# One group of six tiles instead of two in the seven-product form of a feed-forward layer's second product

## The chip, the cores and the metric

The kernel runs on one core of a Trainium2 chip. Each core has a matrix engine (TensorE, PE in the profile; its weight loads are shown apart as PEld), a vector engine (VectorE, DVE), a scalar engine (ScalarE, ACT), GpSimd (POOL) and SyncE (SP). The last two mostly issue DMA transfers here. All engines run their own queue of instructions in order and wait for each other through semaphores. The metric is the device time of one execution in microseconds. In three runs of the kernel before it was 897.86 (median), 897.61 and 958.67.

## What is computed

One layer of a diffusion backbone over 512 latent tokens with 1024 channels and a context of 256 tokens: a normalised and modulated input, a combined projection, a pooling mixer and a two-way chunked recurrent mixer, a gated sum, an output projection, a residual, and then the feed-forward part, in which everything of this case happens:

```python
def _swiglu(h, w_in, w_out):
    g, u = jnp.split(h @ w_in, 2, axis=-1)
    return (jax.nn.silu(g) * u) @ w_out
...
x = x + g1 * mix_lat
x = x + g2 * _swiglu(_modulate(x, norm_ffn[l], sh2, sc2), w_ffn_in[l], w_ffn_out[l])
...
return _rmsnorm(x, norm_final)
```

`h` is 512 x 1024, `w_in` is 1024 x 5632 (gate and up halves of 2816 columns each), `w_out` is 2816 x 1024. The hidden width 2816 makes 22 tiles of 128.

## The kernel before

**Three matmuls for one.** Data are float32. Each operand is split into a rounded high part (a cast on ACT) and the rest (a subtraction on DVE), and a product is made of three matmuls: high by high, high by low, low by high (`mm3`, lines 188 to 190). A token tile is 512 wide; a matmul has 512 or 256 columns.

**Two products.** The first product makes, for a hidden tile j, gate and up values of 128 channels for 512 tokens. The second takes hidden tiles as its contraction and adds `g2` times the sum to the residual `x1` (8 rows of tiles, 128 x 512 each).

**The seven-product form.** `Pair` (line 1066) makes one hidden tile's gate and up values for both token halves as a 2 x 2 block product with seven block multiplications instead of eight. Its weights are loaded as two tiles, `a` (in a buffer `wr`, three of them) and `b` (in a buffer `ur`, two of them), at lines 1018 and 1019; `prepare` makes the split weights of seven block operands: `A11`, `A12`, `A22` (directly, buffers `oh` and `ol`), and the sums `S1`, `S2`, `S3`, `S4` (lines 1049 to 1057, then casts and subtractions into `gh`/`gl` and `wh`/`wl`). For `A12` and `A22`, and for some odd tiles `A11`, the low part is made by a DMA from POOL that adds the weight from DRAM onto the negated high part (line 1036); the last one of a pair is kept as `p["added"]`. Four products are in `front` (A11, S1, S2, A12) and three in `back` (S3, S4, A22). `run` (line 1246) goes through a list of items: the front of an item is interleaved with the back of the one before it, and the next item is prepared meanwhile. One such turn of a `Pair` has seven products of 12 matmuls with 256 columns.

**The seven-product form of the second product.** `Even` and `Odd` (lines 1154 and 1173) are pairs whose results don't become plain hidden tiles: they are combined (`Fed`, buffers `bo`, `nf`, `ev`) into the seven operands that the second product needs. After six such tiles four `Out` items (line 1202) do the second product for two rows each and store the rows, scaled by `g2`, in a DRAM tensor `od` (lines 1236 and 1240).

**The order of the stages in the feed-forward part.** Tiles 0 to 2 are done plainly (class `Half`) in an order written out by hand for TensorE, ACT and DVE (from line 1332). Tile 3 is a `Pair`. Then the plain second product over tiles 0 to 3 (lines 1427 to 1446), whose first three rows are begun while tile 3 is finished; each finished row of `x1` is stored in DRAM (`x1d`) from POOL, since its place in SBUF is used for `Fed`. Then two groups, tiles 4 to 9 and tiles 10 to 15, each three `Even`, three `Odd` and four `Out`. Then six `Pair` items, tiles 16 to 21; during these `x1` comes back from `x1d` on SP's queue (line 1472), and POOL's queue adds the 16 stored rows of both groups to it (line 1477). At last the plain second product over tiles 16 to 21, in token halves, the norm and the output (from line 1508).

**Who sets the order.** Behind the hand-ordered part the order of each engine's queue is made by the compiler's planner from the order in the program, the dependences and its own estimates of durations. `tc.issue_after(ins)` puts the instructions of its block behind `ins` in the queue of their own engine. A planned order isn't changed at run time: an instruction at the head of a queue that waits holds all behind it.

Of the kernel before, what the change touches and what calls it, by code (L numbers as in the profile page):

```python
# [50 lines left out]
def layer_kernel(ctx: ExitStack, tc, xT, cT, w0, w1, wv0, wv, wada_a, wada_b, par, crow, bg, wpool,  # L51
# [4 lines left out]
    pools, homes, stacks = {}, {}, {}  # L56

    shifted = {"ac"}

    def open_pool(name, tags, side="left"):  # L60
        st = ExitStack()
        p = st.enter_context(tc.tile_pool(name=name, bufs=1, side=side, reuse_waits="tile"))
        pools[name] = p
        for t in tags:
            homes[t] = p
        stacks[name] = st

    def close_pool(name):
        stacks.pop(name).close()

    def tl(tag, shape, dtype=F32, bufs=1, align=None):
        cnt[0] += 1
        return homes[tag].tile(shape, dtype, name=f"{tag}_{cnt[0]}", tag=tag, bufs=bufs, align_bytes=align)

    def S(tag, dtype=F32):
        return tl(tag, [P, T], dtype, BUFS[tag], HALFLINE if tag in shifted else LINE)

    ps = ctx.enter_context(tc.tile_pool(name="ps", bufs=4, space=PSUM))
    dram = ctx.enter_context(tc.tile_pool(name="dram", bufs=1, space=DRAM))
# [96 lines left out]
    def split(src, h, l):  # L176
        nc.scalar.copy(h, src)  # L177
        V.tensor_sub(l, src, h.bitcast(F32))  # L178
        return h, l
# [4 lines left out]
    def mm3(dst, wparts, aparts, first=True, last=True, on=False):  # L184

        n = len(wparts)
        for i, ((wh, wl), (ah, al)) in enumerate(zip(wparts, aparts)):
            nc.tensor.matmul(dst, wh, ah, start=first and i == 0, stop=False, skip_group_check=on)  # L188
            nc.tensor.matmul(dst, wh, al, start=False, stop=False, skip_group_check=on)  # L189
            nc.tensor.matmul(dst, wl, ah, start=False, stop=last and i == n - 1, skip_group_check=on)  # L190

    def mm3_low_last(dst, wparts, aparts, first=True, last=True):

        for i, ((wh, _), (ah, al)) in enumerate(zip(wparts, aparts)):
            nc.tensor.matmul(dst, wh, ah, start=first and i == 0, stop=False)  # L195
            nc.tensor.matmul(dst, wh, al, start=False, stop=False)  # L196
        for i, ((_, wl), (ah, _)) in enumerate(zip(wparts, aparts)):
            nc.tensor.matmul(dst, wl, ah, start=False, stop=last and i == len(wparts) - 1)  # L198
# [231 lines left out]

    def queries(h):
        return [conv_part(lat_tile(Q0 + 2 * h + dk), T, 2 * h + dk,
                          [tl("q", [P, T + NEXT], F32R, BUFS["q"], LINE)[:, NEXT:] for _ in range(2)]) for dk in range(2)]

    def keys(h):

# [577 lines left out]
    def prepare(p, wa, wb, n, turns, sent):  # L1014

        a = tl("wr", [P, WMAX], F32, 3)[:, :2 * n]
        b = tl("ur", [P, D], F32, 2)[:, :2 * n]
        nc.sync.dma_start(b, wb)
        p["loaded"] = nc.sync.dma_start(a, wa)

        def tiled(t):
            return t.rearrange("p (k c) -> p k c", c=P) if turns else t

        def parted(t):
            return [tiled(t)[:, e::2] for e in range(2)] if turns else [tiled(t[:, :n]), tiled(t[:, n:])]

        (a11, a12), (a21, a22) = parted(a), parted(b)

        def direct(nm, w, dram):
            h, l = S("oh", F32R)[:, :n], S("ol", F32R)[:, :n]  # L1030
            nc.scalar.copy(tiled(h), w)
            if nm not in sent:
                V.tensor_sub(tiled(l), w, tiled(h).bitcast(F32))
            else:
                nc.scalar.activation(tiled(l), w, AF.Copy, scale=-1.0)  # L1035
                p["added"] = nc.gpsimd.dma_start(tiled(l), dram, accum_op=ALU.add)  # L1036
            p[nm] = ptiles(h, l, 0, n)

        def summed(names, sg, h, l):
            h, l = h[:, :2 * n], l[:, :2 * n]  # L1040
            split(sg, h, l)
            for e, nm in enumerate(names):
                p[nm] = ptiles(h, l, e * n, n)

        yield
        s12 = tl("sg", [P, D], F32, 2, LINE)[:, :2 * n]
        s1, s2 = tiled(s12[:, :n]), tiled(s12[:, n:])
        direct("A11", a11, parted(wa)[0])
        V.tensor_add(s1, a22, a21)
        V.tensor_add(s2, s1, a11)  # L1050
        summed(("S1", "S2"), s12, wide("gh"), wide("gl"))
        yield
        direct("A12", a12, parted(wa)[1])
        yield
        s34 = tl("sg", [P, D], F32, 2, LINE)[:, :2 * n]
        V.tensor_add(tiled(s34[:, :n]), a11, a21)
        V.tensor_add(tiled(s34[:, n:]), s2, a12)
        yield
        summed(("S3", "S4"), s34, *(tl(t, [P, WMAX], F32R, 2, LINE) for t in ("wh", "wl")))
        yield  # L1060
        direct("A22", a22, parted(wb)[1])
        yield
# [3 lines left out]
    class Pair:  # L1066
# [67 lines left out]
            self.done()  # L1134

        def done(self):
            split(self.s, *self.dst)

    class Fed:

# [105 lines left out]
    def run(items, also=lambda it: None):  # L1246

        prev = None
        for it, after in zip(items, items[1:] + [None]):
            f = it.f = it.f or it.front()  # L1250
            if after:
                made(after)
            b = prev.back() if prev else iter(())
            joint = isinstance(it, Out) and not isinstance(prev, Out)
            if not it.begun:
                next(f)
                next(f)
            if joint:
                for _ in b:
                    pass  # L1260
                after.f = after.front()
                next(after.f)
                next(after.f)
                after.begun = True
            next(b, None)
            next(f)
            next(b, None)
            next(f)
            next(b, None)
            also(it)  # L1270
            prev = it
        return prev
# [1 line left out]
    ng2 = small([P, KT], "ng2")  # L1274
    V.tensor_scalar(ng2, g2, -1.0, None, ALU.mult)
    x1d = dram.tile([KT, P, T], F32, name="x1d")
    od = {c0: dram.tile([KT, P, T], F32, name=f"od{c0}") for c0 in (4, 10)}

    for j in range(NW, KT):
        proj_out(j, wo[j], HALF[0])  # L1280
# [120 lines left out]
    def ffn_bank():  # L1401
        turn_[0] += 1
        return banks[turn_[0] % 3]
# [17 lines left out]
    def wchunk(j, c0, c1, dst=None, skip=0, raw=None):  # L1421
        return wload(wffo[j][:, c0 * P:c1 * P], (c1 - c0) * P, dst, skip, raw)[0]
# [1 line left out]

    c1 = NP + 1
    turn_[0] = NP % 3
    for _ in third.f:
        pass  # L1430
    b = third.back()
    next(b)
    next(b)
    wf, af = [], [ffn_bank(), ffn_bank(), banks[3]]
    for j, acc in enumerate(af):
        if j == 2:
            next(b)
        wf.append(wchunk(j, 0, c1, raw=None if j else tl("ur", [P, D], F32, 2)))
        mm3_low_last(acc, wf[j][:NP], act[:NP], last=False)
    for j, acc in enumerate(af):  # L1440
        mm3(acc, wf[j][NP:], act[NP:c1], first=False)
        ffn_out(j, ALL, None, 0, c1, acc)
        nc.gpsimd.dma_start(x1d[j], x1[j])
    for j in range(3, KT):
        ffn_out(j, ALL, wchunk(j, 0, c1), 0, c1)
        nc.gpsimd.dma_start(x1d[j], x1[j])
    close_pool("late4")
    close_pool("late0")
    open_pool("late0", ("bo", "nf", "ev"))
    items, turn = [], itertools.count(NP + 1)  # L1450
    for c0 in (4, 10):
        evens = []
        for j in range(c0, c0 + 6, 2):
            t = next(turn)
            evens.append(Even(j, t, j == c0 + 4, evens[0].turn if evens else t))
            items += [evens[-1], Odd(j + 1, next(turn), evens[-1])]
        items += [Out(j, next(turn), evens, c0, c0 + 6) for j in range(KT // 2)]
    c0, c1 = 16, FT
    plain = [Pair(j, next(turn)) for j in range(c0, c1)]
    back_ = iter(range(KT))  # L1460

    def also(it):
        if it is plain[0]:
            close_pool("late0")
            open_pool("late0", ("act", "before_act", "x1"))
            tl("before_act", [P, NEXT], F32, 1, LINE)
            shifted.add("act")
            x1[:] = [S("x1") for _ in range(KT)]
        elif it in plain:
            with tc.issue_after(plain[min(plain.index(it) + 1, len(plain) - 1)].p["loaded"].ins):  # L1470
                for j in itertools.islice(back_, 2):
                    nc.sync.dma_start(x1[j], x1d[j])
        if it is plain[-2]:
            with tc.issue_after(plain[-1].p["added"].ins):
                for j in range(KT):
                    for c in (4, 10):
                        nc.gpsimd.dma_start(x1[j], od[c][j], accum_op=ALU.add)

    made(items[0])
    for _ in run(items + plain, also=also).back():  # L1480
        pass
    SumSq.banks = banks[4:]

# [136 lines left out]
```

## Time and profile before

The profiled execution took 899.67 us, of which 897.9 lie between its first and its last instruction. Its mean granted TensorE clock is 0.993. Parts of the page and of the views that are used, beside the lines that the prediction shows:

| what | value |
|---|---|
| the three runs, us | 897.61, 897.86, 958.67 |
| the profiled execution, us | 899.67 |
| its span, us | 897.9 |
| matmuls | 6112 |
| DMA over the span | 134.59 MB, mean 150 GB/s |
| DMA share of the 16 engines by SP's queue | 39.0% |
| line 1036 (add of low weights from POOL) | 42 times, 256 KB each |
| line 1477 (add of a stored row to `x1` from POOL) | 16 times, 256 KB each |
| line 1472 (reload of a row of `x1` from SP) | 8 times, 256 KB each, median 8.8 us to landing |

How to read it: lines of the timeline have start, duration, engine, source line, operation, output and inputs, and in brackets the idle time of the engine before it and what ended that time. A line of the waits has the waiting instruction, the one that it waited for, the total in us, how often, and the longest. A line of the windows has, for a stretch, its length, busy time and number of instructions of PE, PEld, DVE, ACT and POOL, the granted clock, the busy share of the DMA engines and GB/s. Matmuls overlap, so their price is the distance from one start to the next, not their duration.

### The profile page before, as it was taken

How to read it: one execution, taken by the hardware profiler on the slowest of the kernel's cores; microseconds unless marked ns; L12 is line 12 of the kernel's file. 1: busy time of each engine (PE TensorE's matmuls, PEld its weight loads, DVE VectorE, ACT ScalarE, POOL GpSimd, SP SyncE). 2: the span in 40 equal slices, each digit the busy share in tenths (PEclk: the TensorE clock that was granted, in tenths of full speed). 3: DMA queues.
4: the chain of work that ended last, by engine and by line, in shares of the span. 5: the costliest groups of instructions: out<-in, count | busy, mean ns of one | idle time of the engine just before them, and what ended most of it. 6: DMA issues, size and time to landing. Idle time of an engine off the chain costs nothing.

```text
span 897.9 us, 15849 instructions
## 1 busy us (share of the span) xinstructions
PE 874.6 (97%) x6112; PEld 805.4 (90%) x6112; DVE 652.8 (73%) x1292; ACT 470.7 (52%) x919; POOL 98.1 (11%) x137
## 2 busy tenths in 40 slices
PE   9999999999999999999999999999999999998896
PEld 8689798899889998889988899879999999998896
DVE  4678677768876788667886659578888788856544
ACT  4454453545445453354545456446757775755442
POOL 0000000110000100001000000031202220221510
PEclk9999999999999999999999999999999999998999
DMA  9863021445352642526354710379637863794862
GB/s 350 317 201 99 25 71 60 164 129 153 106 177 66 194 112 76 191 69 199 98 153 154 276 48 25 94 211 239 142 103 218 218 147 99 223 283 103 181 127 95
DMA packets 48557, 134.59 MB, mean 150 GB/s; under 512 B 5440, under 2 KB 9824, under 8 KB 47456
## 3 DMA queue, kind: packets, MB, share of 16 engines
q1 hardware_dynamic: 38208, 112.06, 39.0%
q0 software_dynamic: 10272, 21.50, 11.7%
q8 instruction: 48, 0.79, 0.3%
q14 instruction: 29, 0.24, 0.1%
HBM read 123.56 MB, written 9.98 MB: 149 GB/s over the span
## 4 chain that ended last, share of the span: by engine, by line
PE 85%; DVE 6%; DMA 3%; ACT 3%; issue 2%; DVEq 0%; SPq 0%; ACTq 0%
PE ps L188 10%; PE ps L189 10%; PE ps L190 10%; PE ps L198 8%; PE ps L195 8%; PE ps L196 8%; PE pat L348 3%; PE ps L579 3%; PE ps L580 3%; PE ps L581 3%; PE pat L189 2%; PE pat L188 2%; PE pat L190 2%; PE pat L793 2%; PE pat L795 2%
## 5 line engine op out<-in xcount | busy, mean ns | idle before, releaser
L195 PE MATMUL ps<-a,wh 128*128 128x512 f32 x272 | 106.5, 392 | 0.0
L196 PE MATMUL ps<-a,wh 128*128 128x512 f32 x272 | 106.3, 391 | 0.0
L158 ACT CAST wh<-wr 128x1024 fp32r<-128x1024 f32 (+3 forms) x69 | 66.7, 969 | 63.4 <-PE ps L196 34.8
L159 DVE TENSOR_TENSOR wl<-wr,wh 128x1024 fp32r<-128x1024 f32 (+3 forms) x69 | 78.2, 1133 | 28.7 <-ACT wh L158 17.5
L198 PE MATMUL ps<-a,wl 128*128 128x512 f32 x272 | 68.0, 391 | 0.0
L196 PEld LDWEIGHTS ps<-a,wh 128*128 128x128 f32 x272 | 51.1, 188 | 10.2
L198 PEld LDWEIGHTS ps<-a,wl 128*128 128x128 f32 x272 | 50.9, 188 | 10.4
L195 PEld LDWEIGHTS ps<-a,wh 128*128 128x128 f32 x272 | 51.1, 188 | 10.1
L188 PE MATMUL ps<-hp,oh 128*128 128x256 f32 x176 | 50.8, 289 | 8.7 <-DVE tmp L1124 8.1
L1036 POOL DMA_DIRECT2D ol<-in_wffi x42 | 37.1, 882 | 146.6 <-ACT ol L1035 61.5
L188 PE MATMUL ps<-hp,gh 128*128 128x256 f32 x176 | 49.8, 283 | 2.9 <-ACT pat L1086 2.9
L190 PE MATMUL ps<-hp,ol 128*128 128x256 f32 x176 | 50.3, 286 | 0.0
L189 PE MATMUL ps<-hp,oh 128*128 128x256 f32 x176 | 50.2, 285 | 0.0
L189 PE MATMUL ps<-hp,gh 128*128 128x256 f32 x176 | 49.0, 278 | 0.0
L190 PE MATMUL ps<-hp,gl 128*128 128x256 f32 x176 | 48.9, 278 | 0.0
L177 ACT CAST gh<-sg 128x1024 fp32r<-128x1024 f32 (+1 forms) x27 | 26.7, 989 | 41.5 <-DVE sg L1050 26.5
L538 DVE SCALAR_TENSOR_TENSOR pb<-pb,crow_s 128x1024 f32<-128x1024 f32 x32 | 39.1, 1239 | 11.9 <-DMA pb<-in_wada_b 11.8
L188 PEld LDWEIGHTS ps<-hp,oh 128*128 128x128 f32 x176 | 34.6, 197 | 9.4 <-DVE tmp L1124 8.5
L793 PE MATMUL pat<-vh,Sp 128*128 128x258 f32 x144 | 41.1, 285 | 0.0
L794 PE MATMUL pat<-vl,Sp 128*128 128x258 f32 x144 | 40.7, 283 | 0.0
L795 PE MATMUL pat<-vh,Sp 128*128 128x258 f32 x144 | 40.7, 282 | 0.0
L178 DVE TENSOR_TENSOR gl<-sg,gh 128x1024 fp32r<-128x1024 f32 (+1 forms) x27 | 30.9, 1145 | 11.6 <-ACT gh L177 11.6
(422 smaller groups left out, 3031.2 us busy)
## 6 DMA issues: line engine op xcount, KB each, us to landing
wr<-in_w SPq DMA_DIRECT2D x42, 512.0 KB, 3.6
pb<-in_wada_b SPq DMA_DIRECT2D x32, 512.0 KB, 4.3
wr<-in_wffi SPq DMA_DIRECT2D x25, 512.0 KB, 4.8
ol<-in_wffi POOLq DMA_DIRECT2D x42, 256.0 KB, 5.8
ur<-in_wffi SPq DMA_DIRECT2D x19, 512.0 KB, 4.2
ada<-in_wada_a SPq DMA_DIRECT2D x8, 1024.0 KB, 9.9
wr<-in_wffo SPq DMA_DIRECT2D x16, 384.0 KB, 5.2
wr<-in_wout SPq DMA_DIRECT2D x8, 512.0 KB, 3.7
```

Of the source, the lines that this page charges most:

```text
L158: nc.scalar.copy(wh, raw[:, :n])
L159: V.tensor_sub(wl, raw[:, :n], wh.bitcast(F32))
L188: nc.tensor.matmul(dst, wh, ah, start=first and i == 0, stop=False, skip_group_check=on)
L189: nc.tensor.matmul(dst, wh, al, start=False, stop=False, skip_group_check=on)
L190: nc.tensor.matmul(dst, wl, ah, start=False, stop=last and i == n - 1, skip_group_check=on)
L195: nc.tensor.matmul(dst, wh, ah, start=first and i == 0, stop=False)
L196: nc.tensor.matmul(dst, wh, al, start=False, stop=False)
L198: nc.tensor.matmul(dst, wl, ah, start=False, stop=last and i == len(wparts) - 1)
L538: V.scalar_tensor_tensor(wa[:, :D], wa[:, :D], 0.5, crow_s, ALU.mult, ALU.mult, accum_out=mods[:, i:i + 1])
L793: nc.tensor.matmul(o, sh_, vh[:, s, :], start=n == 0, stop=False)
L794: nc.tensor.matmul(o, sh_, vl[:, s, :], start=False, stop=False)
L795: nc.tensor.matmul(o, sl_, vh[:, s, :], start=False, stop=n == len(srcs) - 1)
```

## The change

Only tiles 8 to 13 stay in the seven-product form of the second product. The list of first tiles `starts` has one entry, 8, where `(4, 10)` stood. Tiles 3 to 7 are plain `Pair` items, run through `run` like the later ones, and the first plain block of the second product takes the eight tiles 0 to 7, row after row; rows 0 to 5 of `x1` are stored from POOL as before, rows 6 and 7 from SP, behind the preparation of the first even tile. Tiles 14 to 21 are eight `Pair` items (six before), and the last plain block takes these eight tiles, so that a chunk of weights there is 512 KB (384 before).

The stored rows of the one group are no longer added to `x1` in SBUF after it was loaded. They are added in DRAM, `x1d[j] += od[j]`, by POOL's queue during the later plain pairs: in the turns of the second to the seventh of the eight pairs 1, 2, 2, 1, 1 and 1 rows, each behind the last add of low weights (`added`) of the next pair. The eight loads of `x1` are all put into the turn of the last pair but one, behind that `b` load on SP which belongs to the last pair: `loaded` is now the load of `b`, not of `a`.

In `run`, where the first `Out` follows the last `Odd`, the three back products of the odd tile were done together after the first two products of this `Out`; now they alternate: S3, A11 of `Out`, S4, S1 of `Out`, A22. `done` of a pair writes the cast and the subtraction out, with no other operation.

```diff
-        nc.sync.dma_start(b, wb)
-        p["loaded"] = nc.sync.dma_start(a, wa)
+        p["loaded"] = nc.sync.dma_start(b, wb)
+        nc.sync.dma_start(a, wa)
...
         def done(self):
-            split(self.s, *self.dst)
+            nc.scalar.copy(self.dst[0], self.s)
+            self.over = V.tensor_sub(self.dst[1], self.s, self.dst[0].bitcast(F32))
...
             joint = isinstance(it, Out) and not isinstance(prev, Out)
+            if joint:
+                next(b)
             if not it.begun:
                 next(f)
+                if joint:
+                    next(b)
                 next(f)
             if joint:
-                for _ in b:
-                    pass
+                next(b)
                 after.f = after.front()
...
-    for _ in third.f:
+    starts = (8,)
+    turn = itertools.count(NP + 1)
+    plain = [third] + [Pair(j, next(turn)) for j in range(NP + 1, starts[0])]
+    for _ in run(plain).back():
         pass
-    b = third.back()
-    next(b)
-    next(b)
-    wf, af = [], [ffn_bank(), ffn_bank(), banks[3]]
-    for j, acc in enumerate(af):
-        if j == 2:
-            next(b)
-        wf.append(wchunk(j, 0, c1, raw=None if j else tl("ur", [P, D], F32, 2)))
-        mm3_low_last(acc, wf[j][:NP], act[:NP], last=False)
-    for j, acc in enumerate(af):
-        mm3(acc, wf[j][NP:], act[NP:c1], first=False)
-        ffn_out(j, ALL, None, 0, c1, acc)
-        nc.gpsimd.dma_start(x1d[j], x1[j])
-    for j in range(3, KT):
+    turn_[0] = plain[-1].turn % 3
+    c1 = starts[0]
+    for j in range(KT):
         ffn_out(j, ALL, wchunk(j, 0, c1), 0, c1)
-        nc.gpsimd.dma_start(x1d[j], x1[j])
...
+        if j < KT - 2:
+            nc.gpsimd.dma_start(x1d[j], x1[j])
...
+    c0, c1 = starts[-1] + 6, FT
     plain = [Pair(j, next(turn)) for j in range(c0, c1)]
-    back_ = iter(range(KT))
+    items += plain
+    made(items[0])
+    for j in (KT - 2, KT - 1):
+        nc.sync.dma_start(x1d[j], x1[j])
...
-        elif it in plain:
-            with tc.issue_after(plain[min(plain.index(it) + 1, len(plain) - 1)].p["loaded"].ins):
-                for j in itertools.islice(back_, 2):
+        if it in ins[6:] + plain[1:-1]:
+            after = items[items.index(it) + 1].p.get("added")
+            with tc.issue_after(after.ins) if after else ExitStack():
+                for c, j in itertools.islice(rows, 1 + (it in plain[2:4])):
+                    nc.gpsimd.dma_start(x1d[j], od[c][j], accum_op=ALU.add, max_dma_last_dim=2048)
+        if it is plain[-2]:
+            with tc.issue_after(plain[-1].p["loaded"].ins):
+                for j in range(KT):
                     nc.sync.dma_start(x1[j], x1d[j])
-        if it is plain[-2]:
-            with tc.issue_after(plain[-1].p["added"].ins):
-                for j in range(KT):
-                    for c in (4, 10):
-                        nc.gpsimd.dma_start(x1[j], od[c][j], accum_op=ALU.add)
```

More of the change, by code (lines that the diff above doesn't have):

```diff
@@ L58, in layer_kernel @@
     shifted = {"ac"}
+    bufs = dict(BUFS)
     def open_pool(name, tags, side="left"):
@@ L75, in S @@
     def S(tag, dtype=F32):
-        return tl(tag, [P, T], dtype, BUFS[tag], HALFLINE if tag in shifted else LINE)
+        return tl(tag, [P, T], dtype, bufs[tag], HALFLINE if tag in shifted else LINE)
     ps = ctx.enter_context(tc.tile_pool(name="ps", bufs=4, space=PSUM))
@@ L432, in queries @@
         return [conv_part(lat_tile(Q0 + 2 * h + dk), T, 2 * h + dk,
-                          [tl("q", [P, T + NEXT], F32R, BUFS["q"], LINE)[:, NEXT:] for _ in range(2)]) for dk in range(2)]
+                          [tl("q", [P, T + NEXT], F32R, bufs["q"], LINE)[:, NEXT:] for _ in range(2)]) for dk in range(2)]
     def keys(h):
@@ L1276, in layer_kernel @@
     x1d = dram.tile([KT, P, T], F32, name="x1d")
-    od = {c0: dram.tile([KT, P, T], F32, name=f"od{c0}") for c0 in (4, 10)}
+    od = {c0: dram.tile([KT, P, T], F32, name=f"od{c0}") for c0 in (8,)}
     for j in range(NW, KT):
@@ L1422, in wchunk @@
         return wload(wffo[j][:, c0 * P:c1 * P], (c1 - c0) * P, dst, skip, raw)[0]
-    c1 = NP + 1
-    turn_[0] = NP % 3
-    for _ in third.f:
-        pass
-    b = third.back()
-    next(b)
-    next(b)
-    wf, af = [], [ffn_bank(), ffn_bank(), banks[3]]
-    for j, acc in enumerate(af):
-        if j == 2:
-            next(b)
-        wf.append(wchunk(j, 0, c1, raw=None if j else tl("ur", [P, D], F32, 2)))
-        mm3_low_last(acc, wf[j][:NP], act[:NP], last=False)
-    for j, acc in enumerate(af):
-        mm3(acc, wf[j][NP:], act[NP:c1], first=False)
-        ffn_out(j, ALL, None, 0, c1, acc)
-        nc.gpsimd.dma_start(x1d[j], x1[j])
-    for j in range(3, KT):
-        ffn_out(j, ALL, wchunk(j, 0, c1), 0, c1)
-        nc.gpsimd.dma_start(x1d[j], x1[j])
[L1447 to L1451, printed above, removed]
+    starts = (8,)
+    turn = itertools.count(NP + 1)
+    plain = [third] + [Pair(j, next(turn)) for j in range(NP + 1, starts[0])]
+    for _ in run(plain).back():
+        pass
+    turn_[0] = plain[-1].turn % 3
+    c1 = starts[0]
+    for j in range(KT):
+        ffn_out(j, ALL, wchunk(j, 0, c1), 0, c1)
+        if j < KT - 2:
+            nc.gpsimd.dma_start(x1d[j], x1[j])
+    items, ins = [], []
+    for c0 in starts:
         evens = []
@@ L1455, in layer_kernel @@
             evens.append(Even(j, t, j == c0 + 4, evens[0].turn if evens else t))
-            items += [evens[-1], Odd(j + 1, next(turn), evens[-1])]
+            ins += [evens[-1], Odd(j + 1, next(turn), evens[-1])]
+            items += ins[-2:]
         items += [Out(j, next(turn), evens, c0, c0 + 6) for j in range(KT // 2)]
-    c0, c1 = 16, FT
+    c0, c1 = starts[-1] + 6, FT
     plain = [Pair(j, next(turn)) for j in range(c0, c1)]
-    back_ = iter(range(KT))
+    items += plain
+    made(items[0])
+    for j in (KT - 2, KT - 1):
+        nc.sync.dma_start(x1d[j], x1[j])
+    close_pool("late4")
+    close_pool("late0")
+    open_pool("late0", ("bo", "nf", "ev"))
+    rows = iter([(c, j) for c in starts for j in range(KT)])
     def also(it):
@@ L1467, in also @@
             shifted.add("act")
+            bufs["act"] = 2 * (c1 - c0)
             x1[:] = [S("x1") for _ in range(KT)]
-        elif it in plain:
-            with tc.issue_after(plain[min(plain.index(it) + 1, len(plain) - 1)].p["loaded"].ins):
-                for j in itertools.islice(back_, 2):
-                    nc.sync.dma_start(x1[j], x1d[j])
-        if it is plain[-2]:
-            with tc.issue_after(plain[-1].p["added"].ins):
-                for j in range(KT):
-                    for c in (4, 10):
-                        nc.gpsimd.dma_start(x1[j], od[c][j], accum_op=ALU.add)
-    made(items[0])
-    for _ in run(items + plain, also=also).back():
+        if it in ins[6:] + plain[1:-1]:
[6 more added lines that the diff above has]
+                for j in range(KT):
+                    nc.sync.dma_start(x1[j], x1d[j])
+    for _ in run(items, also=also).back():
         pass
```

## The prediction

> **What bounds the kernel now.** I read the page first (engines, then the chain that ended last), then the list of waits of TensorE in the stretch that the change touches (560 to 856 us: the second half of the feed-forward part), then the timelines around the longest of them.
>
> ```profile
> PE 874.6 (97%) x6112; PEld 805.4 (90%) x6112; DVE 652.8 (73%) x1292; ACT 470.7 (52%) x919; POOL 98.1 (11%) x137
> ...
> PE 85%; DVE 6%; DMA 3%; ACT 3%; issue 2%; DVEq 0%; SPq 0%; ACTq 0%
> ```
>
> TensorE is busy for 97% of the span and holds 85% of the chain. Time is therefore made of two things: how many matmul columns are issued, and the few places where PE stands still. The places, in one view (total us, times, longest):
>
> ```profile
> PE ps L188 <- DVE tmp L1124: 8.1, 2, 4.8
> PE ps L188 <- ACT pat L1086: 2.9, 4, 1.6
> PE ps L188 <- ACT bo L177: 1.2, 2, 0.6
> PE ps L188 <- ACT act L177: 1.2, 1, 1.2
> PE ps L188 <- DVE x L1415: 0.6, 1, 0.6
> ```
>
> That is 14.0 us in 296. Two waits make 8.1 of it, and both are followed by a slow stretch of the TensorE clock:
>
> ```profile
> 812.10:816.10 4.00, 4.00 (x19) 4.00 (x20) 3.51 (x6) 3.77 (x7) 0.72 (x1) 0.50 0.05 3
> 850.60:854.00 3.40, 3.40 (x16) 3.40 (x17) 2.86 (x6) 1.39 (x4) 0.95 (x2) 0.52 1.13 203
> ```
>
> The granted clock (third number from the end) is 0.50 and 0.52 there. Now where those two come from. First wait (SyncE's issues, the chain's DMA piece, VectorE, TensorE):
>
> ```profile
> 790.42 0.33 SPq L1018 DMA_DIRECT2D ur<-in_wffi  x1
> 790.84 3.84 SPq L1472 DMA_DIRECT2D x<-x1d  x6
> ...
> 795.58 0.92 SPq L1472 DMA_DIRECT2D x<-x1d  x2
> 799.35 0.33 SPq L1018 DMA_DIRECT2D ur<-in_wffi  x1
> ...
> 815.11 0.33 SPq L1018 DMA_DIRECT2D ur<-in_wffi  x1
> ```
> ```profile
> 799.35 10.83 DMA ur<-in_wffi
> ...
> 842.21 6.03 DMA wr<-in_wffo
> ```
> ```profile
> 794.47 0.69 DVE L1049 TENSOR_TENSOR sg<-ur 128x512 f32<-128x512 f32 x1 [2.11 <-DMA ur<-in_wffi]
> ...
> 795.81 0.42 DVE L1124 TENSOR_TENSOR tmp<-ps,tmp 128x256 f32<-128x256 f32 x1
> ...
> 810.27 0.69 DVE L1049 TENSOR_TENSOR sg<-ur 128x512 f32<-128x512 f32 x1 [7.75 <-DMA ur<-in_wffi]
> ...
> 811.61 0.42 DVE L1124 TENSOR_TENSOR tmp<-ps,tmp 128x256 f32<-128x256 f32 x1
> ...
> 819.21 0.69 DVE L1049 TENSOR_TENSOR sg<-ur 128x512 f32<-128x512 f32 x1 [0.92 <-DMA ur<-in_wffi]
> ...
> 848.91 0.69 DVE L172 TENSOR_TENSOR ol<-wr,oh 128x512 fp32r<-128x512 f32 x1 [3.93 <-ACT oh L171]
> ...
> 850.12 0.42 DVE L1124 TENSOR_TENSOR tmp<-ps,tmp 128x256 f32<-128x256 f32 x1
> ```
> ```profile
> 797.12 0.28 PE L188 MATMUL ps<-hp,oh 128*128 128x256 f32 x1
> ...
> 806.98 0.28 PE L190 MATMUL pat<-hp,ol 128*128 128x256 f32 x1
> 812.08 0.58 PE L188 MATMUL ps<-hp,oh 128*128 128x256 f32 x1 [4.82 <-DVE tmp L1124]
> ...
> 847.04 0.28 PE L190 MATMUL pat<-hp,wl 128*128 128x256 f32 x1
> 850.59 0.58 PE L188 MATMUL ps<-hp,oh 128*128 128x256 f32 x1 [3.27 <-DVE tmp L1124]
> ```
>
> The eight loads of `x1` go out together; the weight load `ur` behind them (799.35) needs 10.83 us, where one on a calm queue (issued 815.11, used 819.21) needs 4.1. VectorE's queue has L1049, which wants that load for a pair two turns on, ahead of L1124, which the present pair wants before its last product. So a late load of a later pair stops PE. The second wait has the same form: the fifth chunk of the closing weights (842.21) needs 6.03 us while POOL adds the stored rows to `x1`; L172 waits for it, and L1124 behind it.
>
> **The change part by part.** Spacing of matmuls, first and last row of two even stretches:
>
> ```profile
> 590.21 0.39 PE L188 MATMUL ps<-act,wh 128*128 128x512 f32 x1
> ...
> 598.60 0.39 PE L189 MATMUL ps<-act,wh 128*128 128x512 f32 x1
> ...
> 613.95 0.28 PE L188 MATMUL ps<-hp,gh 128*128 128x256 f32 x1
> ...
> 620.77 0.28 PE L188 MATMUL ps<-hp,gh 128*128 128x256 f32 x1
> ```
>
> 37 steps in 8.39 us: 0.227 us for 512 columns. 60 steps in 6.82 us: 0.1137 us for 256.
>
> 1. *Columns.* The first product doesn't change: three plain tiles and 19 in seven-product form both times. The second product of a six-tile group in plain form is 8x6x3 = 144 matmuls of 512 columns, 32.7 us; in seven-product form 4x7x3x3 = 252 of 256, 28.7 us. One group fewer in that form: **+4.0 us**, all on PE, nothing hides it. The first plain block grows from 4 tiles to 8 and the last from 6 to 8, as whole matmuls at the same price per column.
> 2. *First wait.* The reload of `x1` is moved behind the last pair's `b` load, so no pair's load stands behind it. 4.82 us of wait go, and the slow clock after it: 4.00 us for 19 matmuls that take 2.16 at 0.1137, so 1.84. **-6.6 us.** What is late next: a calm load leaves L1124 a margin (done 796.23 against the matmul at 797.12: 0.9 us, the smallest of the plain turns), so this wait goes to nothing.
> 3. *Second wait.* It is 3.27 + (3.40 - 16x0.1137 = 1.58) = 4.9 us. The 16 adds at that place go; in their stretch come eight plain reloads (half the transfers) and chunks of 512 KB instead of 384. A 512 KB load on the calm queue took 4.1 us, under the adds a 384 KB load 6.03: the chunk lands 1.9 us earlier at best. I take a wait of 2.0 that stays (3.27 - 1.9 = 1.4 from this, 0.6 for the reloads still in the queue), and no slow clock, since the 1.6 us wait of the list above is followed by none. **-2.9 us**, between -4.9 (gone) and 0 (as late as now).
> 4. *Entry to the even and odd tiles.* 1.6 (L1086) and 0.6 (L1415) belong to it:
>
> ```profile
> 591.79 7.59 SPq L1019 DMA_DIRECT2D wr<-in_wffi  x3
> ```
>
> The raw buffers of the short 4-tile chunks come free late, so the `a` loads of the first even and odd tile go out only at 591.79, 10 us before they are used. With 8 tiles each chunk has 24x0.227 = 5.4 us of PE time and three raw buffers, so those loads go some 16 us ahead. I take 1.8 of the 2.2 off: **-1.8 us**, between -2.2 and 0. The last two rows of `x1` are stored from SP instead of POOL: each waits for its L1415, and SP's next weight loads queue behind it; if they do so in the wrong order, one load is 4 us late and the gain is lost, hence the 0.
> 5. *Second group's own waits* (one 0.6 at L177, one 0.5 at L1086): **-1.1 us**, between -1.1 and 0.
> 6. *Joint order.* The last odd tile's back products are put between the first ones of `Out`. S3 (12 matmuls, 1.4 us) now stands where PE waits 0.6 for the cast of the last even tile: **-0.6 us**, between -0.6 and +0.6 (S3 is asked for 2 us earlier).
> 7. *Handover to tiles 4 to 7.* The 1.2 us wait (act L177) before the first block goes, since seven tiles (21x0.227 = 4.8 us) cover the last cast. In its place the hand-ordered part ends with a pair whose successor's splits are not done: S1 and S2 need two sums, a cast and a subtraction, some 3.5 us, with two products (2.8 us) before them. **0 us**, between -1.2 and +1.2.
> 8. *Rows added in DRAM.* Nothing like it is in the trace; the nearest is an add into SBUF:
>
> ```profile
> q0 software_dynamic: 10272, 21.50, 11.7%
> ...
> DMA to landing us min/median/max: 4.7/6.8/11.7
> ...
> 825.10:834.70 9.60, 9.60 (x86) 9.60 (x85) 5.13 (x10) 5.40 (x11) 1.75 (x2) 1.00 0.50 96
> ```
>
> By the first row 256 KB of POOL's queue holds the 16 DMA engines for 0.117x897.9/82 = 1.3 us. A turn of a plain pair is 9.6 us with the DMA half idle (0.50), so one row or two (2.6 us) fit. Each is issued behind the pair's own add, and both after that turn's `ur` load. **0 us**, between 0 and +9.8 (third rival).
> 9. *x1[7] on SP.* Its load waits for the last row, issued at the start of the last turn and landed 4.7 to 11.7 us later; the closing chunks queue behind it on SP. Now the fifth chunk goes out at 842.21, some 8 us after the turn starts, because its buffer isn't free earlier; this hides it. Without that cover: the excess of 11.7 over 8, 3.7 us. **0 us.** The longer splits (1.05 and 1.23 us instead of 0.84 and 0.96) lie under 5.4 us of PE per chunk. `done` is the same two instructions written out: 0.
>
> Sum: +4.0 - 6.6 - 2.9 - 1.8 - 1.1 - 0.6 = **-9.0 us**. The profiled execution took 899.67 us (span 897.9), 1.8 above the median of the runs; 890.7 against it is **888.9** against the median 897.86.
>
> **The rivals.** *Both long waits go.* The compiler's planner writes the order outside the hand-ordered part; if L1124 comes ahead of L172, step 3 gives 4.9 and the time is 886.9. For it: the longer chunk arrives later in any plan, so the planner has less reason to put L172 first. Against: it did so before.
>
> *The reload moves the stall.* The change doesn't do what it says: the eight loads of `x1`, 2 MB at once, stand before a closing chunk instead of a pair's load. If that chunk takes the 10.83 us of the load now behind them instead of 6.03, the second wait grows by 4.8 and step 3 gives nothing: 888.9 + 2.9 + 4.8 = 896.6. For it: the same burst did this at 799. Against: most rows are ready early, and the loads can be spread over three turns.
>
> *The rows make each turn's load late.* If the whole engine time of an add falls on the next `ur` load, at 1.9 us each (16 adds in the 30 us that they take now), a turn with one row has L1124 1.9 - 0.9 = 1.0 us late, a turn with two 2.9: 4x1.0 + 2x2.9 = 9.8 us, 898.7 in all, just slower than before. It decides from 1.9 us an add on. Against it: the load at 790.42, with `x1` loads issued 0.4 us behind it, was used at 794.47, as quickly as the calm one. The Trainium skill, "DMA: Bandwidth & Descriptors", section "Queues, rings and completion order", says that each DMA engine goes round the queues that have work, a packet at a time; by that rule POOL's rows would share with SP's load however late they are issued, which is this rival in its mild form. The trace agrees with it only where the queues were full (10.83 us), not at 790.42.
>
> **How the numbers follow.** Forecast 0.5 (888.9), both waits gone 0.2 (886.9), reload moves the stall 0.2 (896.6), rows make loads late 0.1 (898.7). The open ends of steps 4 to 7 are some 3 us to either side. The range that leaves out 2 in 10 is 882 to 897; the forecast alone has 884 to 893. What a measurement of this kernel tells from no change is about 2%, 18 us: faster means under 879.9. All waits of the list and both slow stretches together are 17.4 us, less 4.0 for the columns: even that gives 884.5. So faster 0.04, slower 0.03 (two rivals together and a planner's mishap), within 2% 0.93.
>
> **What would show it.** Right: no PE wait of over 1 us and clock 1.00 through the eight closing pairs' turns; one wait of about 2 us at L1124 near the last pair's end; 192 matmuls of 512 columns in the first block in 43.6 us; the wait at L1086 after that block under 0.5 us. Wrong: a `ur` load of over 6 us beside the rows (third rival), a closing chunk of about 10 us (second), a clock of 0.5 anywhere behind 560 us, or waits of several us between tiles 3 and 8, which step 7 puts at nothing.

## The result

| | median us | lowest to highest | runs |
|---|---|---|---|
| before | 897.74 | 897.05 to 958.67 | 4 |
| changed | 888.16 | 887.77 to 890.41 | 4 |

The medians lie 9.6 us apart. The ratio of the undisturbed runs is 0.9906, 95% interval 0.9885 to 0.9928, which is 0.9% or some 8.4 us less. (The run of 958.67 is in a slower state, as is one of 957.52 with a granted clock of 0.848 among those of two groups below; both are left out of the ratios.) 888.9 had been forecast. The sum was right; several of its terms were not, and that their errors nearly cancelled was luck.

The page of the changed kernel, engines and chain:

```profile
PE 875.0 (98%) x6052; PEld 804.8 (91%) x6052; DVE 631.5 (71%) x1232; ACT 454.0 (51%) x867; POOL 83.9 (9%) x117
...
PE 90%; issue 4%; DVE 2%; DMA 2%; ACT 1%; POOL 0%; DVEq 0%; POOLq 0%; ACTq 0%
```

The first line is each engine's busy time, share and instructions, the last the chain's shares. TensorE is busy for 98% of the span. Its waits in the same part of the kernel (line, what was waited for, total us, times, longest):

```profile
PE ps L189 <- ACT pat L1087: 2.3, 2, 2.0
PE pat L191 <- DMA ol<-in_wffi: 2.1, 2, 1.8
PE ps L189 <- ACT oh L1032: 0.5, 1, 0.5
PE ps L190 <- DVE bo L179: 0.3, 1, 0.3
```

(Lines behind 1017 are one further down than before: L1125 is the old L1124, L1087 the old L1086.) 5.2 us of waits stand where 14.0 stood. The line of 8.1 us, `L188 <- DVE tmp L1124`, is gone altogether, not only its first half. In its place are two single waits of 1.8 and 2.0 us. Where they lie, and the clock behind each (stretch, busy times and counts of PE, PEld, DVE, ACT and POOL, granted clock, DMA share, GB/s):

```profile
580.33 0.28 PE L190 MATMUL pat<-hp,oh 128*128 128x256 f32 x1
582.38 0.38 PE L191 MATMUL pat<-hp,ol 128*128 128x256 f32 x1 [1.77 <-DMA ol<-in_wffi]
...
819.98 0.28 PE L191 MATMUL ps<-hp,wl 128*128 128x256 f32 x1
822.22 0.39 PE L189 MATMUL ps<-hp,gh 128*128 128x256 f32 x1 [1.96 <-ACT pat L1087]
```
```profile
583.90:587.10 3.20, 3.20 (x17) 3.20 (x16) 0.91 (x3) 1.31 (x3) 0.87 (x1) 0.50 1.09 301
822.20:826.20 4.00, 3.98 (x20) 3.98 (x21) 1.77 (x4) 1.31 (x2) 0.27 (x1) 0.57 0.85 144
770.00:818.00 48.00, 48.00 (x423) 48.00 (x422) 32.46 (x52) 28.79 (x53) 13.08 (x15) 1.00 0.96 220
```

The first wait is at the handover to tile 4: a product needs a low part that POOL's add has not yet brought. The second is in the last pair's turn but one. Third row: before it, 48 us of closing pairs pass with PE busy throughout at clock 1.00, so the late load of a pair is really gone; but the DMA engines are 0.96 busy in that stretch. What this does to the closing chunks is seen on SP, POOL, the chain and ACT:

```profile
797.11 9.64 SPq L1479 DMA_DIRECT2D x<-x1d  x6
806.85 2.80 SPq L156 DMA_DIRECT2D wr<-in_wffo  x2
```
```profile
807.11 1.19 POOL L1475 DMA_DIRECT2D x1d<-od  x1
```
```profile
809.33 7.72 DMA wr<-in_wffo
```
```profile
817.13 1.05 ACT L178 CAST gh<-wr 128x1024 fp32r<-128x1024 f32 x1 [7.25 <-DMA wr<-in_wffo]
```

SP sends five loads of `x1`, then waits until 806.4 for the sixth, which needs its row added; two closing chunks come behind it, and POOL's next row between them. The second chunk takes 7.72 us. ACT's queue has its cast ahead of everything else and stands for 7.25 us; L1087, a copy that TensorE needs, is behind it.

What the stages cost beyond their columns, from the traces: the distance from each matmul's start to the next, less 0.443 ns a column (0.1135 us for 256), summed over the stage. The last column is the changed kernel in another profiled execution, on another chip, where no slow clock followed the two waits.

| stage | before | changed | changed again |
|---|---|---|---|
| tile 3 (to 7) and the first plain block | 3.4 | 5.8 | 3.4 |
| entry to even and odd tiles | 2.9 | 0.4 | 0.5 |
| first group | 3.8 | 3.3 | 2.8 |
| second group, with its entry | 2.9 | none | none |
| closing pairs | 13.6 | 4.5 | 5.1 |
| sum | 26.6 | 14.0 | 11.8 |

12.6 and 14.8 us less, against 4.0 us more of columns: 8.6 and 10.8, and the spans fell by 9.3 and 11.3. Not all of this excess is waiting: in some stretches matmuls of 256 columns stand 0.118 us apart instead of 0.1135, at a granted clock of 1.00, and these stretches differ between executions of one kernel. The same 45 matmuls of the `Out` items took 5.30 us in the changed kernel's first profiled execution (from 733.53) and 5.10 in its second (from 731.25). From 560 to 872 us all spacings of up to 0.126 us add 2.3 to 4.7 us over 0.1135 a matmul, by execution, so a difference of 1 or 2 us between two traces can be this alone; its cause is not known.

### The profile page after: what moved, and what is told of

The parts are those of the page before. It is cut to its first block, busy times and chain, and to the rows that moved or that the text cites. A ratio compares the mean times of both kernels' runs of the same rounds, so it can differ in the third digit from the quotient of the medians.

```text
span 888.6 us, 15515 instructions
## 1 busy us (share of the span) xinstructions
PE 875.0 (98%) x6052; PEld 804.8 (91%) x6052; DVE 631.5 (71%) x1232; ACT 454.0 (51%) x867; POOL 83.9 (9%) x117
## 4 chain that ended last, share of the span: by engine, by line
PE 90%; issue 4%; DVE 2%; DMA 2%; ACT 1%; POOL 0%; DVEq 0%; POOLq 0%; ACTq 0%
PE ps L189 12%; PE ps L190 12%; PE ps L191 12%; PE ps L199 8%; PE ps L197 8%; PE ps L196 8%; PE pat L349 3%; PE ps L580 3%; PE ps L581 3%; PE ps L582 3%; PE pat L794 2%; PE pat L190 2%; PE pat L189 2%; PE pat L795 2%; PE pat L796 2%
## 5 line engine op out<-in xcount | busy, mean ns | idle before, releaser
L159 ACT CAST wh<-wr 128x1024 fp32r<-128x1024 f32 (+2 forms) x70 | 71.8, 1025 | 81.4 <-PE ps L197 34.9
L160 DVE TENSOR_TENSOR wl<-wr,wh 128x1024 fp32r<-128x1024 f32 (+2 forms) x70 | 84.2, 1203 | 33.7 <-ACT wh L159 21.8
L196 PEld LDWEIGHTS ps<-a,wh 128*128 128x128 f32 x272 | 51.1, 188 | 10.1
L189 PE MATMUL ps<-act,wh 128*128 128x256 f32 (+1 forms) x155 | 51.4, 332 | 0.0
L190 PE MATMUL ps<-act,wh 128*128 128x256 f32 (+1 forms) x155 | 51.3, 331 | 0.0
L191 PE MATMUL ps<-act,wl 128*128 128x256 f32 (+1 forms) x155 | 51.3, 331 | 0.0
L189 PE MATMUL ps<-hp,oh 128*128 128x256 f32 x176 | 49.6, 283 | 0.5 <-ACT oh L1032 0.5
L1037 POOL DMA_DIRECT2D ol<-in_wffi x40 | 35.3, 883 | 155.6 <-ACT tmp L1122 67.6
L190 PE MATMUL ps<-hp,oh 128*128 128x256 f32 x176 | 49.4, 281 | 0.0
L539 DVE SCALAR_TENSOR_TENSOR pb<-pb,crow_s 128x1024 f32<-128x1024 f32 x32 | 39.2, 1240 | 10.8 <-DMA pb<-in_wada_b 10.8
```

What stands on the lines that cost most here:

```text
L159: nc.scalar.copy(wh, raw[:, :n])
L160: V.tensor_sub(wl, raw[:, :n], wh.bitcast(F32))
L539: V.scalar_tensor_tensor(wa[:, :D], wa[:, :D], 0.5, crow_s, ALU.mult, ALU.mult, accum_out=mods[:, i:i + 1])
```

## The experiments

The runs were made in four batches, each on one chip and each with runs of the kernel before; across batches the ratios to that kernel are compared. Its medians were 897.74, 899.47, 899.35 and 899.58.

### The rows left out

```diff
-                    nc.gpsimd.dma_start(x1d[j], od[c][j], accum_op=ALU.add, max_dma_last_dim=2048)
+                    pass
```

> Leaves the eight adds of stored rows out (the output lacks the middle six hidden tiles). In the changed kernel one wait of 2.0 us is left before the last pair: ScalarE's queue stands 7.25 us at the cast of a closing chunk that landed 7.7 us after its issue. Theory A (the rows: x1's loads on SP wait for rows, one closing chunk is held behind them and then two chunks, a load and a row come in a cluster): without rows that chunk lands in about 4 us, the wait goes, 886.0 us (888.1 less 2.0), 884.5 if a slow clock goes with it. Theory B (the eight loads of x1 themselves fill the DMA queue): the wait stays above 1 us, 887.5 or more. Third rival of the prediction (rows make the turn's load late): 1 us a turn comes off, 882 or less.

884.3 us, ratio 0.9828 [0.9809, 0.9846]. The wait of 2 us is gone; the longest wait is now 0.6:

```profile
PE ps L189 <- ACT pat L1087: 0.9, 3, 0.4
PE pat L191 <- DMA ol<-in_wffi: 0.6, 1, 0.6
PE ps L189 <- ACT oh L1032: 0.5, 1, 0.5
PE ps L190 <- DVE bo L179: 0.3, 1, 0.3
```

So the adds of the rows, set at nothing in step 8, cost some 5 to 7 us (0.9828 against 0.9888, the changed kernel when it was run again, and 0.9906 the first time; each with some 0.002 of uncertainty). That the rows make the wait holds, as theory A has it, but the gain is larger than its 2.0 to 3.7 us, and the second chunk takes 5.6 us to land, not the 4 expected. The first chunk behind the eight loads takes 10.1 us even here, with no wait of TensorE behind it.

### The reload behind the `a` load again

```diff
-        p["loaded"] = nc.sync.dma_start(b, wb)
-        nc.sync.dma_start(a, wa)
+        nc.sync.dma_start(b, wb)
+        p["loaded"] = nc.sync.dma_start(a, wa)
```

> The changed kernel with the loads of x1 put behind the a load of the last pair again, some 15 us earlier, so that two b loads stand behind loads of x1 on SP. Step 2 of the prediction (the place of the reload made the first wait): a b load is late again by 4 us or more, a wait at L1125 of 3 to 6 us and a slow clock, 892 to 896 us. Rival (the place doesn't matter, the first wait went because POOL's adds or the second group went): 888.1, within 1 us.

892.96 us, ratio 0.9925 [0.9903, 0.9947], with the old wait back:

```profile
PE ps L189 <- DVE tmp L1125: 3.5, 1, 3.5
```
```profile
777.53 7.89 SPq L1479 DMA_DIRECT2D x<-x1d  x3
785.52 0.38 SPq L1019 DMA_DIRECT2D ur<-in_wffi  x1
```
```profile
785.52 8.46 DMA ur<-in_wffi
```

Three loads of `x1` hold SP for 7.89 us (they wait for their rows), and the pair's load behind them takes 8.46. Step 2's mechanism, with the second form of it, a held queue, on top.

### Three rows of `x1` loaded from POOL

```diff
-                    nc.sync.dma_start(x1[j], x1d[j])
+                    (nc.sync if j < 5 else nc.gpsimd).dma_start(x1[j], x1d[j])
```

> Rows 5 to 7 of x1 are loaded from POOL's queue behind the last row's add instead of from SP; nothing else. SP then has no load that waits for a row in front of closing chunks. Theory A with the hold as its cause: the chunk that went out at 806.85 goes some 7 us earlier, the next one (its buffer is free at 809) lands in 5 us instead of 7.7, the 2.0 us wait falls below 0.5: 886.2 us. If it is the rows' traffic and not the hold: the wait stays at 1.5 to 2.5 us, 888. Theory B: stays as well.

887.53 us, ratio 0.9865 [0.9841, 0.9888]. SP is not held any more, but the wait stays (first row), and ACT still stands for that chunk (second):

```profile
PE ps L189 <- ACT pat L1087: 1.9, 2, 1.6
```
```profile
815.02 1.05 ACT L178 CAST gh<-wr 128x1024 fp32r<-128x1024 f32 x1 [6.68 <-DMA wr<-in_wffo]
```

That chunk goes out at 807.79, no earlier in its turn than in the changed kernel (12.5 us behind the turn's `ur` load, there 12.6), and still takes 7.2 us to land; the one before it, no longer held, goes out at 798.54 and takes 11.6. So the held queue isn't what makes the chunk late. The traffic beside it is what is left; whose traffic, the next experiment tells.

### The rows added early

```diff
-        if it in ins[6:] + plain[1:-1]:
+        if it in plain[:4]:
...
-                for c, j in itertools.islice(rows, 1 + (it in plain[2:4])):
+                for c, j in itertools.islice(rows, 2):
```

With the changed kernel itself beside it:

> The changed kernel unchanged, as the yardstick for the three beside it on the same chip, and to see how its two waits of some 2 us and the slow clock behind them vary from one execution to the next: 886 to 890 us.

> All eight rows are added in the first four of the eight closing pairs' turns, two in each, so that none runs beside the reload and the closing chunks. Theory A' (the 2.0 us wait near the last pair comes from the rows' traffic beside a closing chunk; taking the hold on SP away left it at 1.6): the wait falls below 0.5, 2.0 us less than the changed kernel, 1.7 more where a slow clock goes with it. Rival (it is the rows' number, wherever they stand): a b load is late in one of the first four turns and a wait of 1 us or more comes there; no gain.

The changed kernel: 888.97 us, 0.9888 [0.9865, 0.9912]. Rows early: 884.72, 0.9836 [0.9809, 0.9862], 4.2 us less. Its waits at L1087 are four of at most 0.7 us, and a small one comes where the rows now are:

```profile
PE ps L189 <- ACT pat L1087: 1.8, 4, 0.7
...
PE ps L189 <- DVE tmp L1125: 0.5, 1, 0.5
```

The chunk that ACT stood for, issued at 809.40, lands in 5.6 us instead of 7.7. The number of rows is the same; so nearly all that they cost comes from where they stand, as far as ratios of two batches tell (0.9836 here, 0.9828 without rows). Theory A' holds; its rival has the 0.5 us. The gain of 4.2 us is more than the wait (1.6 us in the trace of the changed kernel beside it) can account for. The profiled execution is the slowest of its four (886.86), so its trace can't show where the rest comes from.

### The handover to tile 4

```diff
+    plain[1].sent = ("A22",)
     for _ in run(plain).back():
```

> Only the low part of A12 of tile 4 is made by a subtraction on VectorE instead of an add from POOL. In the changed kernel the 1.9 us wait at tile 4 (TensorE for that add, landed 7.0 us after its issue) stands against step 7 of the prediction, which had the handover at nothing. If the add is its cause, 1.9 us go and VectorE's 0.7 us are hidden: 1.5 to 2 us less than the changed kernel. Rival (another product of that handover is late next): less than 0.7 us.

886.06 us, 0.9857 [0.9831, 0.9884], 2.9 us below the changed kernel beside it. In the stretch of the handover only waits of 0.4 us are left. The add was the cause, and nothing else was late behind it. The gain is above the 1.1 us that the unchanged kernel's profile beside it shows for this wait, so some of it is not explained by that wait alone; intervals of 2 us and more leave this open.

### Two groups, with and without the rows

```diff
-    starts = (8,)
+    starts = (4, 10)
...
-                for c, j in itertools.islice(rows, 1 + (it in plain[2:4])):
+                for c, j in itertools.islice(rows, 1 if it in ins else 3 if it in plain[1:3] else 2):
```

> The changed kernel with both groups of six tiles in the seven-product form again (tiles 4 to 9 and 10 to 15), all else as changed: rows added in DRAM (16 of them, three or two a turn at the end), reload behind the last b load, new joint order. Step 1 of the prediction (the plain form costs 4.0 us of columns, a group's own waits 1.1 us): 888.1 - 4.0 + 1.1, and the short first block brings the entry's wait of up to 2.2 us back: 885 to 887.5 us. Rival (a group in the seven-product form costs more beside its columns than it saves, and that is where the gain is from): 890 or more.

897.01 us, 0.9973 [0.9951, 0.9996]. Sixteen rows leave little of the gain; two long waits stand at the end again, the first as in the changed kernel, the second as in the one before:

```profile
PE ps L189 <- ACT pat L1087: 5.8, 6, 3.0
PE ps L189 <- DVE tmp L1125: 4.3, 2, 4.1
```

The same with the adds left out:

> Two groups in the seven-product form, and no row is added at all (the output lacks the middle twelve hidden tiles). Against the kernel without rows and one group (0.9828 of the kernel before) it shows step 1 clean of the rows: 4.0 us of columns less, 1.1 to 2 us of a group's own waits and up to 1.5 us at the entry more: 1 to 3 us faster than that, ratio 0.980 to 0.982. Rival (the group's own cost is above its columns' gain): not faster, ratio 0.983 or more.

889.06 us, 0.9888 [0.9866, 0.9910], against 0.9828 for one group without rows: 5 us slower, though it has 4.0 us of columns less. The rival was right. Excess over the columns by stage, worked out as in the table above, one group to two: handover and first block 3.0 to 5.2, entry 0 to 0.9, first group 3.3 to 3.8, second group and its entry none to 4.1, closing pairs 1.3 to 3.2; sum 7.6 to 17.2. So a second group costs about as much of its own (4.1) as its 4.0 us of columns. Of the rest, 3.1 us lie around the short first block, in the handover and the entry; some 1.3 of them are a slow clock (0.53 from 580.2 to 583.0) behind a wait of 1.77 us. Another 1.9 us come in the closing pairs and are not explained.

### The old joint order

```diff
             if not it.begun:
                 next(f)
                 next(f)
             if joint:
                 for _ in b:
                     pass
```

> The changed kernel with the joint order of before (two products of the first Out, then the odd tile's three back products). Step 6 of the prediction: a wait of 0.6 us at a cast into bo in front of the first Out's first product comes back, 0.6 us slower than the changed kernel (ratio 0.989 to 0.990 on chips where that has 0.9888 to 0.9906), and what the changed kernel has there now (0.3 us at a subtraction into bo) goes. Rival (the wait only moved): the sum of both is the same, no difference.

887.96 us, 0.9870 [0.9849, 0.9891]. The wait of 0.6 came back in front of the first `Out` (`ACT bo L178`), the 0.3 at the subtraction went:

```profile
PE ps L189 <- ACT bo L178: 0.6, 1, 0.6
```

The time did not get worse (0.9870 against 0.9888 and 0.9906 in other batches). By the trace the new order gains 0.3 us, by the time nothing that these runs can tell.

### The kernel before, with one thing changed

```diff
-        elif it in plain:
-            with tc.issue_after(plain[min(plain.index(it) + 1, len(plain) - 1)].p["loaded"].ins):
-                for j in itertools.islice(back_, 2):
-                    nc.sync.dma_start(x1[j], x1d[j])
         if it is plain[-2]:
+            with tc.issue_after(plain[-1].p["loaded"].ins):
+                for j in range(KT):
+                    nc.sync.dma_start(x1[j], x1d[j])
```

(and `loaded` the load of `b`):

> The kernel before with one thing changed: all eight loads of x1 go behind the last pair's b load, as in the changed kernel; both groups, the adds into x1 and the joint order stay. Step 2 of the prediction: the wait of 4.8 us and the slow clock at 812 go (6.6 us), and the second wait stays or grows, since loads, adds and closing chunks now come together: 4.9 to 10 us in place of 4.9, so 891 to 896 in place of 897.7, ratio 0.993 to 0.998. Rival (the late b load is not the x1 loads' doing): the first wait stays, ratio 0.999 to 1.001.

891.61 us, 0.9910 [0.9882, 0.9939]: 8.0 us less from the place of the eight loads alone, with an interval of 5.5 to 10.6. One wait is left at L1124, the second, without a slow clock behind it in this execution:

```profile
PE ps L188 <- DVE tmp L1124: 3.2, 1, 3.2
```
```profile
842.40:846.40 4.00, 3.97 (x34) 3.97 (x35) 3.31 (x7) 2.01 (x5) 0.41 (x1) 1.00 1.12 203
```

And the other half, the 16 adds left out of the kernel before:

```diff
-                        nc.gpsimd.dma_start(x1[j], od[c][j], accum_op=ALU.add)
+                        pass
```

> The kernel before without the 16 adds of stored rows into x1 (the output lacks the middle twelve hidden tiles); all else stays. Step 3 of the prediction: the second wait (3.3 us and 1.6 us of slow clock) is the adds' doing and goes, the first one stays: 4.9 us less, ratio 0.9945. Rival (a closing chunk is late by its buffer, whatever runs beside it): less than 2 us.

895.09 us, 0.9951 [0.9930, 0.9971], 4.5 us. The first wait stays at 4.8, the second falls to 0.4:

```profile
PE ps L188 <- DVE tmp L1124: 5.2, 2, 4.8
```

### Rows early and the handover together

> The changed kernel with the rows added early (0.9836 of the kernel before, where the changed one had 0.9888) and tile 4's low part on VectorE (0.9857) together. If both waits are apart, their gains add up: 4.2 + 2.9 = 7.1 us below the changed kernel, ratio 0.981. If one only makes room for the other: 0.983 to 0.985.

883.88 us, 0.9829 [0.9803, 0.9855]. The lowest of the kernels that compute the whole layer, 15.7 us under the kernel before on that chip. The interval holds both 0.981, the sum of the two gains, and 0.983, the overlap, and it can't be told from the rows added early alone (0.9836) either. In this part of its trace no wait of over 0.5 us is left:

```profile
PE ps L189 <- ACT pat L1087: 1.0, 3, 0.4
PE ps L189 <- ACT oh L1032: 0.5, 1, 0.5
PE ps L190 <- DVE bo L179: 0.3, 1, 0.3
PE pat L191 <- DMA ol<-in_wffi: 0.3, 1, 0.3
```

Whether the two gains add up is open. Its profiled execution (886.44) is the slowest of its four (882.83 the fastest); stretches with matmuls 0.118 us apart make some 2 us (4.7 us from 560 to 872, against 2.6 with the rows early alone).

## Why the prediction was right

By its own signs it was right in part. The first block came out as said, no pair's load was late, and the wait behind the block fell to 0.3 us. But a clock of about 0.5 came back twice, which it had named as a sign of being wrong, and the wait of 2 us stood elsewhere and had another cause.

1. *Columns, +4.0.* The 192 matmuls of the first block took 43.5 us (43.6 forecast). The term stands.
2. *First wait, -6.6.* Gone in the changed kernel; back when the loads are moved ahead again (3.5 us of wait, ratio 0.9925); gone from the kernel before when they alone are moved (8.0 us). Shown from both sides. It is the largest term of the gain.
3. *Second wait, -2.9.* The mechanism was right: without the adds it falls from 3.3 to 0.4 and 4.5 us go, 4.9 forecast for the whole. In the changed kernel nothing of it stays at L1125, so the term was 2.0 too small. There the planner's order has changed too, as the rows under the rivals show. Without the adds and in the old order 0.4 us stayed; no run has the old order with the changed kernel's transfers, so how much of the missing 2.0 us is the order's doing stays open. A wait of about 2 us near the last pair was forecast and came, but at another instruction, on another engine's queue, from another cause (step 8).
4. *Entry, -1.8.* Mis-sized: 2.9 of excess became 0.4. The 0 end, SP's stores holding its loads, did not come.
5. *Second group's waits, -1.1.* Mis-sized: only two waits of the list had been counted. The excess of that stage and its entry was 2.9, and in the kernel with two groups and no rows about 4.
6. *Joint order, -0.6.* 0.3 by the trace, nothing by the time.
7. *Handover, 0.* Right as a sum (3.4 before, 3.4 and, with a slow clock, 5.8 after), wrong as a picture: a wait of 1.1 to 1.8 us stands there, and taking it away gained 2.9 us.
8. *Rows, 0.* This step failed. It said that one or two rows fit into a turn because the DMA was 0.50 busy. That row, 825.10 to 834.70, is of a turn late in the kernel before, in which no pair's weights are loaded any more. With a turn's own loads it is 0.72 (the kernel without rows, 768 to 795 us), and with the rows 0.96. The share alone does not decide, though: with the rows early it is 0.97 from 758 to 794, and no wait there is over 0.7 us. What the step left out is what stands beside a row when it moves: the transfer that lands late is not the next `ur` load, as the third rival had it, but a closing chunk. Cost some 5 us or more, 4.2 of which go when the rows stand earlier.
9. *x1[7] on SP, 0.* SP was held, and from x1[5] on, earlier than said; that this did not make the wait is shown by the reload from POOL, which left it at 1.6. Whether it cost anything else, the ratio there (0.9865) is too close to 0.9888 to tell.

Taken by the measured sizes, 4.0 - 6.6 - 4.9 - 2.5 - 2.9 - 0.3, and 3.7 for the new wait with its slow clock, make -9.5, where -9.6 was measured between the medians, -8.4 by the ratio. The agreement is no proof of each term: the sum has the slow clock behind the second wait, which only some executions have, leaves out the one behind the handover, and mixes terms from traces with terms from times. In the forecast 1.8 us too little for the second group, 0.7 for the entry and 2.0 for the second wait stood against 3.7 that were missing for the rows.

Of the rivals, *both waits go* came in its mechanism: both waits at L1124 are gone, and in the last pair's turn VectorE now has L1125 ahead of L173, the split of the chunk, where L172 (848.91) stood ahead of L1124 (850.12) before. That was its condition:

```profile
831.32 0.42 DVE L1125 TENSOR_TENSOR tmp<-ps,tmp 128x256 f32<-128x256 f32 x1
832.31 1.29 DVE L173 TENSOR_TENSOR ol<-wr,oh 128x512 fp32r<-128x512 f32 x2 [0.57 <-ACT oh L172]
```

TensorE goes on to the next product at 832.20, before L173 starts, so with L1125 behind L173 it would have waited. The time of this rival, 886.9, did not come, since the rows made a new wait. The reload moving the stall (896.6) came in kind, a closing chunk of 7.72 us instead of the 10.83 it reckoned with, at 2 us instead of 4.8, with the rows as its cause. The third, in which a page of the Trainium skill was weighed ("DMA: Bandwidth & Descriptors", section "Queues, rings and completion order"): VectorE's waits for the four `ur` loads that were issued just ahead of a row are small,

```profile
771.88 0.69 DVE L1050 TENSOR_TENSOR sg<-ur 128x512 f32<-128x512 f32 x1 [0.78 <-DMA ur<-in_wffi]
...
781.60 0.69 DVE L1050 TENSOR_TENSOR sg<-ur 128x512 f32<-128x512 f32 x1 [1.32 <-DMA ur<-in_wffi]
...
790.86 0.69 DVE L1050 TENSOR_TENSOR sg<-ur 128x512 f32<-128x512 f32 x1 [0.97 <-DMA ur<-in_wffi]
...
801.36 0.69 DVE L1050 TENSOR_TENSOR sg<-ur 128x512 f32<-128x512 f32 x1 [1.86 <-DMA ur<-in_wffi]
```

with no wait of PE behind any of them. They took 3.7 to 4.6 us to land, those of the kernel without rows 3.7 to 4.0. The sharing that the page tells of shows little in them, and plainly in loads that are issued while rows are under way, as the chunk at 809.33 (7.72 us).

## What to carry to other kernels

Where a queue's order is fixed ahead, a late transfer stops TensorE through whichever instruction stands behind its user, on any engine; look for what else is in the DMA queues in the few us before it was issued, and move that, before touching columns. Read the room that a transfer has from a stretch with the same loads: a free DMA in the last turns says nothing of the turns before. And a block of plain matmuls is worth more than its columns if it lies where the next stage must be prepared: with 8 tiles in the first block the handover and the entry cost 3.0 to 4.6 us beyond their columns, with 4 tiles 4.8 to 6.3, slow clocks left out.

## What the runs showed of the hardware

The clock fell to half behind waits that were shorter than the ones that did it before. The Trainium skill, "TensorE: Matmul & The Clock Gate", section "HAM oscillation — how this bites in real kernels", gives idle gaps of over about 3.4 us as the abstract rule. Here 0.50 and 0.57 follow waits of 1.77 and 1.96 us (the first slow stretch begins 1.5 us after the wait's end), and 1.00 follows one of 3.2 us in the kernel before with late loads (its row of 842.40 to 846.40 above). Over all profiled executions, from 555 to 872 us, no wait of up to 1.70 us has a slow clock behind it; those of 1.77 (twice), 1.96, 3.27, 3.52, 4.07 and 4.8 (twice) us have one, and those of 3.02 and 3.19 have none. In the changed kernel's other profiled execution the second wait was 1.55 us long and ended at 820.42; the 4 us behind it:

```profile
820.40:824.40 4.00, 3.98 (x33) 3.99 (x34) 2.41 (x4) 2.28 (x4) 0.27 (x1) 1.00 0.85 134
```

So a wait of 1.8 to 3.3 us cost either its own length or some 1.7 us more, and one execution doesn't tell which: the changed kernel's execution with both slow stretches took 890.41 us, its others in that batch 887.77 to 888.24.

An add of 256 KB from DRAM to DRAM took 6.3 to 10.3 us from issue to landing, the adds into SBUF of the kernel before 4.7 to 11.7 (medians 8.4 and 6.8), each beside other traffic. The changed kernel's eight rows:

```profile
DMA to landing us min/median/max: 6.3/8.4/10.3
```
